# Features split where they are made, and matmul operands at one place modulo 256 bytes

## The chip, the cores and the metric

The kernel runs on one core of a Trainium2 chip, in one launch. The metric is device time in microseconds (us) of one execution. The core has five engines that work side by side, each through its own instructions in order: TensorE (PE) multiplies matrices, with its weight loads shown apart as PEld; VectorE (DVE), ScalarE (ACT) and GpSimd (POOL) work on elements; SyncE (SP) issues most DMA transfers. On-chip memory is a set of 128 partitions, and "place" below means the byte offset of a tile within its partition.

## The reference

Two layers of a decoder trunk act on 1024 prompt tokens and 8 x 8 sample tokens, 1088 rows of width 1024. Layer 0 mixes with an RG-LRU block, layer 1 with an HGRN2 block; each is followed by a feed-forward block with a convolution of width 3 over time (ConvFFN, 2816 features) and each half ends in a layer norm of `ALPHA * x + f(x)`:

```python
def conv_ffn(x, buf, w_in, cw, cb, w_out):
    gate, up = jnp.split(x @ w_in, 2, axis=-1)
    gc, new_buf = causal_dwconv(gate, buf, cw, cb)
    return (jax.nn.gelu(gc) * up) @ w_out, new_buf

def trunk(x, ...):
    for i in range(DEPTH):                       # 2
        mix = rglru_mixer(x, ...) if i % 2 == 0 else hgrn2_mixer(x, ...)
        x = layer_norm(ALPHA * x + mix, ln_g[i, 0], ln_b[i, 0])
        f, fbuf = conv_ffn(x, ffn_conv[i], ffn_w_in[i], ffn_conv_w[i], ffn_conv_b[i], ffn_w_out[i])
        x = layer_norm(ALPHA * x + f, ln_g[i, 1], ln_b[i, 1])
```

All is float32. Besides the rows of both streams, the last states of the mixers and of the convolutions are returned.

## The kernel before, in words

**Split products.** Each operand of a large product is held as two parts in the type fp32r: hi, the value cast, and lo, what the cast left over (value minus hi). A product is three matmuls: hi with hi, hi with lo, lo with hi. A weight tile of 2 x 1024 columns (hi, lo) is made out of a raw tile that a DMA has filled: ACT casts hi, another engine (`run["lo"]`, mostly POOL) subtracts for lo. `convert` does this for a whole tile (lines L220, L221), `convert_part` for half a tile of 512 columns (L189, L190). `pump` asks for the next raw load and makes one such conversion; `fill` and `flush` run small closures that wait in the list `pend`.

**Memory.** `xa` holds the split input of a product as [hi 1088 columns, lo 1088 columns] per block of 128 features. It is one tile under three names: `x` by feature block, `xc[0..3]` as inputs of the up-projection, `yv[0..7]` as eight blocks of features for the down-projection. A tile `x45` holds `xc[4]` and `xc[5]`, later `yv[8..11]`; a tile `x6` holds `xc[6]`. `z` holds the 1088 rows of the residual in float32, nine row tiles of 1024 columns. During the up-projection those rows lie in DRAM (`zsave`), and `z` is cut into eight work slots of 1152 columns (`zslots`). The base weight tiles are `wb0..2` with the raws `raw0, raw1`; each stage adds its own from a pool (`wxf` and `rawf` in the up-projection, `wxb` in the down-projection, `wr` in `mix_out`, which is the output projection of a mixer).

**Order.** The program's order on each engine is written out by hand (`manual_schedule`): a list of steps, each with its weight blocks and a function, run one after another by `run_steps`. An engine takes its instructions in the order in which the functions issue them.

**Up-projection.** The 22 feature blocks are taken in pairs, p = 0 to 10. Each pair has a step `gates` and a step `ups`. Both run `products`: the 2 x 2 blocks of weights and inputs are multiplied in seven products instead of eight, with inputs `xc[0..6]` that are sums of input quarters (`to_sums` writes them), and the seven results are added up in the work slots on evacuation (L1164, L1177 to L1179). Each product comes in two column chunks of 288 and 256 columns (`HCH`; the first holds 32 sample columns), so a step has 7 x 2 x 4 x 3 = 168 matmuls (L1159). The first `gates` step runs `products_first`. Between the products `fills` place other work by (product, chunk): in `ups` the convolution of the gates of the same pair (DVE, then a GELU on ACT); in the next pair's `gates` step `y_mul` of the two blocks, the product of gate and up on DVE, whose result is stored to DRAM (`ysave`, L1230 and L1231) in float32 and whose slots go back. In the last `ups` step there follow `y_load` of blocks 0 to 11 (L1236), `y_part` of the first six, and after the products `y_mul` of the last pair.

**Split on arrival.** `y_part` splits a loaded block in place: two casts on ACT (L1242: 1024 and 64 columns) and two subtractions (L1243), on POOL for odd positions and on DVE for even ones.

**Turn.** A step `turn` between up- and down-projection allocates `wxb`, loads the nine row tiles of `z` back from `zsave` (`load_z`, L653) and puts `y_part` of blocks 6 to 11 into `pend`.

**Down-projection.** The features are taken in four groups (`GROUPS`: blocks 0 to 5, 6 to 11, 12 to 17, 18 to 21). For each group and each half n of the 1024 output columns the nine row tiles m are taken in order; a row tile is 6 x 3 matmuls of 512 columns into one PSUM bank (L1260 to L1262; the sample tile m = 8 takes hi and lo of its 64 rows in one operand and needs 6 x 2, L1265 and L1266), and `resid` adds the bank to `z` on DVE (L463). In the first half of group 0 the first three tiles begin with four blocks each. After a group's second half the group after the next is loaded into the free places, and its `y_part` goes into `pend`. The last group runs within the layer norm.

**What lies where.** The tiles are allocated in order, so that sizes set the places: `xa`, `z`, `gb`, `ident`, `ones`, then 5312 bytes of small tables, then the raws and the base weight tiles. In the up-projection's pool the table `fs` (1584 bytes) stands ahead of `rawf` and `wxf`.

Of the kernel before, what the change touches and what calls it, by code (L numbers as in the profile page):

```python
# [10 lines left out]
F32 = mybir.dt.float32  # L11
FR = mybir.dt.float32r
# [32 lines left out]
HCH = ((0, HD + 256), (HD + 256, 256))  # L45
TW = 1152
# [14 lines left out]
def hawk_hgrn2_convffn_deepnorm_kernel(  # L61
# [27 lines left out]
    ones = cp.tile([P, P], F32, name="ones")  # L89
    ptr = cp.tile([P, KT, 41], F32, name="ptr")  # L90
# [8 lines left out]
    raws = [cp.tile([P, 1024], F32, name=f"raw{i}", tag=f"raw{i}") for i in range(2)]  # L99
    wbase = [cp.tile([P, 2, 1024], FR, name=f"wb{i}", tag=f"wb{i}") for i in range(3)]  # L100
# [266 lines left out]
    def to_sums(mp):  # L367


        if mp < 4:  # L370
            t0, n, ms = HD + mp * P, P, (mp, mp + 4)
# [10 lines left out]
        else:  # L382
            t0, n, ms = 0, HD, (NT - 1,)
# [13 lines left out]
        def put(c, src, eng):  # L397
            hi, lo = (xc[c][:, :, h, t0:t0 + n] for h in range(2))
            act.copy(hi, src)
            eng.tensor_tensor(lo, src, hi, ALU.subtract)  # L400

        def hi_lo(c):
            return (xc[c][:, :, h, t0:t0 + n] for h in range(2))
# [191 lines left out]
    def params_r():  # L595
# [6 lines left out]
        tmp = m1.tile([P, 6, KT], F32, name="ptmp")  # L602
        a, u, q, zz, s, t = (tmp[:, i] for i in range(6))
# [35 lines left out]
    def y_split(m, ks=range(0, KT)):  # L639
        k = slice(ks[0], ks[-1] + 1)  # L640
        if m < NT - 1:
            tk = slice(m * P, (m + 1) * P)
            dst = xm[:, m // 4, k, :, HD + (m % 4) * P:HD + (m % 4 + 1) * P]
            hi, lo = dst[:, :, 0], dst[:, :, 1]
        else:
            tk = slice(SEQ, U)
            hi, lo = ys[:, k, 0], ys[:, k, 1]
# [7 lines left out]
    def mix_out(phase, w, z_src, li, es, early=None):  # L655
# [4 lines left out]
        def prod_part(ps, m, ks, ws, ends=(0, KT - 1)):  # L660
            if m < NT - 1:
                xt = xm[:, m // 4, :, :, HD + (m % 4) * P:HD + (m % 4 + 1) * P]
                for k in ks:
# [3 lines left out]
                    pe.matmul(ps, lhsT=xt[:, k, 0], rhs=wh, start=(k == ends[0]), stop=False)  # L667
                    pe.matmul(ps, lhsT=xt[:, k, 0], rhs=wl, start=False, stop=False)  # L668
                    pe.matmul(ps, lhsT=xt[:, k, 1], rhs=wh, start=False, stop=(k == ends[1]))  # L669
# [108 lines left out]
    def more_weights(es, name, n, kind, side=None):  # L778
        m3 = es.enter_context(tc.tile_pool(name=name, bufs=1, side=side, reuse_waits="tile"))
        wfree[kind].extend(m3.tile([P, 2, 1024], FR, name=f"{name}{i}", tag=f"{name}{i}") for i in range(n))  # L780

# [1149 lines left out]
```

## Time and profile before

| | us |
|---|---|
| three runs | 2563.02, 2563.65, 2564.53 |
| median | 2563.65 |
| the profiled execution, its own time | 2563.38 |
| its span | 2561.6 |
| mixer 0 and what stands ahead of it | 0 to 345 |
| up-projection of layer 0 | 345 to 822 |
| down-projection of layer 0 | 822 to 1060 |
| mixer 1 | 1060 to 1795 |
| up-projection of layer 1 | 1795 to 2272 |
| down-projection of layer 1, with the last layer norm | 2272 to 2561.6 |

The profile comes from one profiled execution. The profile's page gives the busy time of each engine, its share of the span and the number of instructions. Rows of a timeline give the start and length of an instruction, or of a run of equal ones (`x24`), in us from the span's start, its engine, line, operation, `out<-in` by tile names, and shape. Rows of a group give a busy time and the mean length of one instruction in ns. Rows of waits give idle time in us that ended with a release by the named work: the sum, the number of waits, the longest. Rows of a window give its length, the busy time of PE, PEld, DVE, ACT and POOL with instruction counts, the share of full speed that the TensorE clock was granted, the busy share of the DMA engines, and GB/s. Matmuls are pipelined: one of 512 columns is shown with 0.39 us, while the next starts 0.23 us after it; the pace is read from start to start.

### The profile page before, as it was taken

How to read it: one execution, taken by the hardware profiler on the slowest of the kernel's cores; microseconds unless marked ns; L12 is line 12 of the kernel's file. 1: busy time of each engine (PE TensorE's matmuls, PEld its weight loads, DVE VectorE, ACT ScalarE, POOL GpSimd, SP SyncE). 2: the span in 40 equal slices, each digit the busy share in tenths (PEclk: the TensorE clock that was granted, in tenths of full speed). 3: DMA queues.
4: the chain of work that ended last, by engine and by line, in shares of the span. 5: the costliest groups of instructions: out<-in, count | busy, mean ns of one | idle time of the engine just before them, and what ended most of it. 6: DMA issues, size and time to landing. Idle time of an engine off the chain costs nothing. (4 is left out here: it accounts for less than half of the span.)

```text
span 2561.6 us, 39936 instructions
## 1 busy us (share of the span) xinstructions
PE 2496.6 (97%) x16055; PEld 2311.5 (90%) x16055; DVE 1539.0 (60%) x2360; ACT 952.7 (37%) x1659; POOL 1366.3 (53%) x1154
## 2 busy tenths in 40 slices
PE   9999999999999999999999999999999999999997
PEld 8999889999999788799999999878999999988886
DVE  5897476565556322558858485977656565561327
ACT  4776243333334011344444353454423333330113
POOL 2544178888886333025444453623888888862320
PEclk9999999999999999999999999999999999999999
DMA  4114122223224422122111111122222322263112
GB/s 134 42 46 163 42 78 68 85 76 94 85 68 165 144 102 100 41 76 59 51 34 43 51 43 50 44 87 104 75 85 68 102 85 68 85 232 131 59 38 73
DMA packets 205839, 209.79 MB, mean 82 GB/s; under 512 B 13201, under 2 KB 167953, under 8 KB 205614
## 3 DMA queue, kind: packets, MB, share of 16 engines
q1 hardware_dynamic: 205654, 207.25, 25.2%
q8 instruction: 126, 2.06, 0.3%
q14 instruction: 59, 0.48, 0.1%
HBM read 159.61 MB, written 47.61 MB: 81 GB/s over the span
## 5 line engine op out<-in xcount | busy, mean ns | idle before, releaser
L221 POOL TENSOR_TENSOR wb<-raw,wb 128x1024 fp32r<-128x1024 f32 (+1 forms) x75 | 203.2, 2713 | 520.0 <-ACT wb L220 388.9
L1159 PE MATMUL ps_f<-xa,wb 128*128 128x288 f32 x3024 | 390.6, 288 | 1.3 <-ACT z L1179 1.3
L1164 DVE TENSOR_TENSOR z<-z,ps_f 128x256 f32<-128x256 f32 (+2 forms) x520 | 186.2, 380 | 340.7 <-PE ps_f L1159 278.7
L1159 PEld LDWEIGHTS ps_f<-xa,wb 128*128 128x128 f32 x3024 | 384.5, 188 | 1.7 <-ACT z L1179 1.7
L304 PE MATMUL ps_in<-xa,wb 128*128 128x384 f32 (+3 forms) x912 | 306.3, 336 | 10.9 <-ACT y8h L1453 5.9
L305 PE MATMUL ps_in<-xa,wb 128*128 128x384 f32 (+3 forms) x912 | 299.7, 329 | 0.3 <-DVE xa L362 0.3
L306 PE MATMUL ps_in<-xa,wb 128*128 128x384 f32 (+3 forms) x912 | 299.6, 329 | 0.0
L1159 PE MATMUL ps_f<-x,wb 128*128 128x256 f32 (+1 forms) x2304 | 299.1, 289 | 0.0
L1159 PEld LDWEIGHTS ps_f<-x,wb 128*128 128x128 f32 x2304 | 294.1, 189 | 0.2
L463 DVE SCALAR_TENSOR_TENSOR z<-z,ps_fo 128x512 f32<-128x512 f32 x128 | 87.5, 686 | 301.1 <-PE ps_fo L1262 287.3
L190 POOL TENSOR_TENSOR wb<-raw,wb 128x512 fp32r<-128x512 f32 x124 | 177.8, 1443 | 67.9 <-ACT wb L189 66.5
L304 PEld LDWEIGHTS ps_in<-xa,wb 128*128 128x128 f32 x912 | 173.0, 190 | 15.2 <-ACT y8h L1453 7.3
L1210 DVE SCALAR_TENSOR_TENSOR z<-z,ptf 128x1104 f32<-128x1104 f32 x88 | 181.8, 2066 | 1.6
L190 POOL TENSOR_TENSOR wb<-rawf,wb 128x512 fp32r<-128x512 f32 x106 | 148.2, 1403 | 55.2 <-ACT wb L189 49.3
L305 PEld LDWEIGHTS ps_in<-xa,wb 128*128 128x128 f32 x912 | 172.9, 190 | 1.3 <-DVE xa L362 0.7
L306 PEld LDWEIGHTS ps_in<-xa,wb 128*128 128x128 f32 x912 | 172.6, 189 | 0.7
L189 ACT CAST wb<-raw 128x512 fp32r<-128x512 f32 x124 | 75.3, 623 | 201.7 <-POOL raw L185 57.4
L220 ACT CAST wb<-raw 128x1024 fp32r<-128x1024 f32 (+1 forms) x79 | 77.5, 984 | 153.6 <-issue 52.9
L1159 PE MATMUL ps_f<-xa,wxf 128*128 128x288 f32 (+1 forms) x1008 | 133.6, 288 | 0.0
L1260 PE MATMUL ps_fo<-wb,xa 128*128 128x512 f32 x320 | 127.4, 398 | 5.2 <-DVE z L463 5.2
L189 ACT CAST wb<-rawf 128x512 fp32r<-128x512 f32 x106 | 64.7, 623 | 180.3 <-POOL rawf L185 65.9
L1159 PEld LDWEIGHTS ps_f<-xa,wxf 128*128 128x128 f32 x1008 | 129.6, 189 | 0.0
(522 smaller groups left out, 5794.1 us busy)
## 6 DMA issues: line engine op xcount, KB each, us to landing
raw<-in_ffn_w_in_dram SPq DMA_DIRECT2D x48, 512.0 KB
ysave<-z SPq DMA_DIRECT2D x44, 512.0 KB
rawf<-in_ffn_w_in_dram SPq DMA_DIRECT2D x40, 512.0 KB
raw<-in_hg_w_in_dram SPq DMA_DIRECT2D x32, 512.0 KB
xa<-ysave SPq DMA_DIRECT2D x28, 544.0 KB
zsave<-z SPq DMA_DIRECT2D x24, 512.0 KB
rawf<-in_ffn_w_out_dram SPq DMA_DIRECT2D x24, 512.0 KB
z<-zsave SPq DMA_DIRECT2D x24, 512.0 KB
```

The lines of the kernel that those rows point to most:

```text
L189: act.copy(w[:, 0], src)
L190: run["lo"].tensor_tensor(w[:, 1], src, w[:, 0], ALU.subtract)
L220: act.copy(w[:, 0, :n], raw[:, :n])
L221: run["lo"].tensor_tensor(w[:, 1, :n], raw[:, :n], w[:, 0, :n], ALU.subtract)
L304: pe.matmul(ps[:, :n], lhsT=wh, rhs=xh, start=(k == 0), stop=False)
L305: pe.matmul(ps[:, :n], lhsT=wh, rhs=xl, start=False, stop=False)
L306: pe.matmul(ps[:, :n], lhsT=wl, rhs=xh, start=False, stop=(k == KT - 1))
L463: dve.scalar_tensor_tensor(zz, zz, a, ps, ALU.mult, ALU.add, accum_out=stat[:, m, n:n + 1] if acc else None)
L1159: pe.matmul(ps[:, :n], lhsT=l, rhs=r, start=(kk == 0 and i < 4 and l is wh and r is xh), stop=(kk == 3 and l is wl), skip_group_check=(i > ...
L1164: dve.tensor_tensor(d, s, pv(ps), ALU.add)
L1210: dve.scalar_tensor_tensor(c[:, :L], gs[:, i:i + L], w[:, i:i + 1], c[:, :L], ALU.mult, ALU.add)
L1260: pe.matmul(ps, lhsT=yh, rhs=wh, start=a, stop=False)
```

## The change

1. **Where features are split.** `y_part` is gone. `y_hi` (two ACT casts per block) and `y_lo` (two subtractions) stand behind `y_mul` in the next pair's `gates` step, the subtractions on DVE; for the last pair they follow its `y_mul` after the products, the subtractions on POOL. `ysave` has twice the columns and holds prompt hi, sample hi, sample lo and prompt lo; `y_load` loads that. `y_mul` of the second block moves from place (1, 1) to (1, 0).
2. **The turn.** In the last `ups` step only blocks 0 to 5 are loaded, and behind product (5, 1) the row tiles 6, 7 and 8 of `z` (`FREE`); the `turn` step loads the other six row tiles, then blocks 6 to 11. The down-projection takes the row tiles in the order 6, 7, 8, 0 to 5.
3. **Places.** `wb0..2` and the raws are allocated right behind `ones`, ahead of the small tables; `wxf` is the first tile of its pool; four unused tiles fill up (64, 64, 96 and 32 bytes). `xa`, `x45`, the weight tiles and the raws thereby stand at one place modulo 256 bytes.
4. **Columns.** The prompt and sample columns within a hi or lo part of the inputs get another order: `HX` gives the first column of each chunk, apart for hi and lo, and `h_cols` the columns of a row tile. `to_sums`, `y_split` (split for `mix_out`) and `mix_out` use them. An unused helper `put` is taken out.

```diff
+HX = ((256, 0), (0, HD + 256))
+
+def h_cols(q, h):
+    return HX[0][h] if q == 4 else HX[0][h] + HD + q * P if q < 2 else HX[1][h] + (q - 2) * P
...
     ones = cp.tile([P, P], F32, name="ones")
+    wbase = [cp.tile([P, 2, 1024], FR, name=f"wb{i}", tag=f"wb{i}") for i in range(3)]
+    raws = [cp.tile([P, 1024], F32, name=f"raw{i}", tag=f"raw{i}") for i in range(2)]
     ptr = cp.tile([P, KT, 41], F32, name="ptr")
...
+    cp.tile([P, 16], F32, name="pad")
-    ysave = dpool.tile([NF * P, U], F32, name="ysave")
-    raws = ...
-    wbase = ...
+    ysave = dpool.tile([NF * P, 2 * U], F32, name="ysave")
...
         def hi_lo(c):
-            return (xc[c][:, :, h, t0:t0 + n] for h in range(2))
+            return (xc[c][:, :, h, h_cols(mp, h):h_cols(mp, h) + n] for h in range(2))
...
         tmp = m1.tile([P, 6, KT], F32, name="ptmp")
+        m1.tile([P, 16], F32, name="pad1")
...
             if m < NT - 1:
-                xt = xm[:, m // 4, :, :, HD + (m % 4) * P:HD + (m % 4 + 1) * P]
+                xt, xl = (xm[:, m // 4, :, h, h_cols(m % 4, h):h_cols(m % 4, h) + P] for h in range(2))
...
-        more_weights(mo["r"], f"wr{phase}", 2, "r", "right")
+        more_weights(mo["r"], f"wr{phase}", 2, "r", "right", 24)
...
+    FREE = (6, 7, 8)
...
-            fs_["fs"] = fp.tile([P, NF, 18], F32, name=f"fs{li}")
+            wfree["x"].append(fp.tile([P, 2, 1024], FR, name=f"wxf{li}"))
             fs_["raw"] = [fp.tile([P, 1024], F32, name=f"rawf{li}{i}", tag=f"rawf{i}") for i in range(2)]
-            wfree["x"].append(fp.tile([P, 2, 1024], FR, name=f"wxf{li}"))
+            fs_["fs"] = fp.tile([P, NF, 18], F32, name=f"fs{li}")
+            fp.tile([P, 8], F32, name=f"padf{li}")
...
-                    xh, xl = (xc[i][:, kk, h, c0:c0 + n] for h in range(2))
+                    xh, xl = (xc[i][:, kk, h, HX[c][h]:HX[c][h] + n] for h in range(2))
...
-            sp.dma_start(ysave[f * P:(f + 1) * P, NS:], c[:, :SEQ])
-            sp.dma_start(ysave[f * P:(f + 1) * P, :NS], up[:, U:U + NS])
-            T.put(c, up)
+        def y_hi(f):
+            c, up = yst["c", f], yst[f]
+            uf = up.bitcast(FR)
+            act.copy(uf[:, :SEQ], c[:, :SEQ])
+            act.copy(uf[:, SEQ:U], up[:, U:U + NS])
+
+        def y_lo(f, eng):
+            c, up = yst["c", f], yst[f]
+            cf, uf = c.bitcast(FR), up.bitcast(FR)
+            eng.tensor_tensor(cf[:, :SEQ], c[:, :SEQ], uf[:, :SEQ], ALU.subtract)
+            eng.tensor_tensor(uf[:, U:U + NS], up[:, U:U + NS], uf[:, SEQ:U], ALU.subtract)
+            sp.dma_start(ysave[f * P:(f + 1) * P, U + NS:], c[:, :SEQ])
+            sp.dma_start(ysave[f * P:(f + 1) * P, :U + NS], up[:, :U + NS])
+            fs_["T"].put(c, up)

         def y_load(f, i):
-            sp.dma_start(yv[i][:, U:].bitcast(F32), ysave[f * P:(f + 1) * P])
-
-        def y_part(f, i):
-            y = yv[i]
-            for hi, lo in ((y[:, :SEQ], y[:, U + NS:]), (y[:, SEQ:U], y[:, U:U + NS])):
-                act.copy(hi, lo.bitcast(F32))
-                (pool if i % 2 else dve).tensor_tensor(lo, lo.bitcast(F32), hi, ALU.subtract)
+            sp.dma_start(yv[i].bitcast(F32), ysave[f * P:(f + 1) * P])
...
-                    fills = {(0, 1): [lambda: y_mul(f0 - 2)], (1, 1): [lambda: y_mul(f1 - 2)]}
+                    fills = {(0, 1): [lambda: y_mul(f0 - 2)], (1, 0): [lambda: y_mul(f1 - 2)],
+                             (2, 0): [lambda: y_hi(f0 - 2), lambda: y_hi(f1 - 2)],
+                             (3, 0): [lambda: y_lo(f0 - 2, dve)], (3, 1): [lambda: y_lo(f1 - 2, dve)]}
...
-                    for i in range(3, 6):
-                        fills.setdefault((i, 1), []).extend([lambda i=i, j=j: y_load(2 * i + j, 2 * i + j) for j in range(2)])
-                        fills[i, 1].extend([lambda i=i, j=j: y_part(2 * i + j - 6, 2 * i + j - 6) for j in range(2)])
+                    fills.setdefault((5, 1), []).append(lambda: load_z(z_back, FREE))
                 products(b, (u_place(f0), u_place(f1)), fills)
                 if p == NP - 1:
                     y_mul(f0)
                     y_mul(f1)
+                    for f in (f0, f1):
+                        y_hi(f)
+                        y_lo(f, pool)
...
-            load_z(lambda m: zsave[m * P:m * P + rows_of(m)])
+            load_z(z_back, [m for m in range(NT) if m not in FREE])
             load_gb(li, 1)
-            pend.extend([lambda i=i: y_part(i, i) for i in range(6, 12)])
+            for i in range(6, 12):
+                y_load(i, i)
...
-                        for m in range(first):
-                            prod_part(banks[m], m, grp, ws, range(4))
-                        for m in range(NT):
+                        ms = FREE + tuple(m for m in range(NT) if m not in FREE)
+                        for m, ps in zip(ms, banks):
+                            prod_part(ps, m, grp, ws, range(4))
+                        for i, m in enumerate(ms):
...
-                                    pend.append(lambda f=g2 + j, i=j2 + j: y_part(f, i))
```

More of the change, by code (lines that the diff above doesn't have):

```diff
@@ L370, in to_sums @@
         if mp < 4:
-            t0, n, ms = HD + mp * P, P, (mp, mp + 4)
+            n, ms = P, (mp, mp + 4)
             q = []
@@ L642, in y_split @@
             tk = slice(m * P, (m + 1) * P)
-            dst = xm[:, m // 4, k, :, HD + (m % 4) * P:HD + (m % 4 + 1) * P]
-            hi, lo = dst[:, :, 0], dst[:, :, 1]
+            hi, lo = (xm[:, m // 4, k, h, h_cols(m % 4, h):h_cols(m % 4, h) + P] for h in range(2))
         else:
@@ L666, in prod_part @@
                     wl = wt[:, 1, (k % 2) * 512:(k % 2 + 1) * 512]
-                    pe.matmul(ps, lhsT=xt[:, k, 0], rhs=wh, start=(k == ends[0]), stop=False)
-                    pe.matmul(ps, lhsT=xt[:, k, 0], rhs=wl, start=False, stop=False)
-                    pe.matmul(ps, lhsT=xt[:, k, 1], rhs=wh, start=False, stop=(k == ends[1]))
+                    pe.matmul(ps, lhsT=xt[:, k], rhs=wh, start=(k == ends[0]), stop=False)
+                    pe.matmul(ps, lhsT=xt[:, k], rhs=wl, start=False, stop=False)
+                    pe.matmul(ps, lhsT=xl[:, k], rhs=wh, start=False, stop=(k == ends[1]))
             else:
@@ L776, in hawk_hgrn2_convffn_deepnorm_kernel, with more_weights @@
     mo = {}
-    def more_weights(es, name, n, kind, side=None):
+    def more_weights(es, name, n, kind, side=None, pad=0):
         m3 = es.enter_context(tc.tile_pool(name=name, bufs=1, side=side, reuse_waits="tile"))
         wfree[kind].extend(m3.tile([P, 2, 1024], FR, name=f"{name}{i}", tag=f"{name}{i}") for i in range(n))
+        if pad:
+            m3.tile([P, pad], F32, name=f"pad{name}")
     def mix_out_open(phase):
         mo["r"] = ExitStack()
-        more_weights(mo["r"], f"wr{phase}", 2, "r", "right")
+        more_weights(mo["r"], f"wr{phase}", 2, "r", "right", 24)
     def sums_open(es):
@@ L1109, in products_first @@
                             wh, wl = (w[:, a, kk * P:(kk + 1) * P] for a in range(2))
-                            xh, xl = (xc[i][:, kk, a, c0:c0 + n] for a in range(2))
+                            xh, xl = (xc[i][:, kk, a, HX[c][a]:HX[c][a] + n] for a in range(2))
                             for l, r in ((wh, xh), (wh, xl), (wl, xh)):
@@ L1307, in ups, with z_back @@
                     y_mul(f1)
+                    for f in (f0, f1):
+                        y_hi(f)
+                        y_lo(f, pool)
             stepf(phase, [(in_blk(W, f0 * P), in_blk(W, f1 * P))], gates, None if p else "q")
             stepf(phase, [(in_blk(W, DFF + f0 * P), in_blk(W, DFF + f1 * P))], ups)
+        def z_back(m):
+            return zsave[m * P:m * P + rows_of(m)]
         def turn(_):
@@ L1332, in fn @@
                         banks = [sbank("ps_fo") for _ in range(first)]
-                        for m in range(first):
-                            prod_part(banks[m], m, grp, ws, range(4))
-                        for m in range(NT):
-                            if m < first:
-                                prod_part(banks[m], m, grp, ws, range(4, grp[1]))
-                                resid(m, n, banks[m], True)
+                        ms = FREE + tuple(m for m in range(NT) if m not in FREE)
+                        for m, ps in zip(ms, banks):
+                            prod_part(ps, m, grp, ws, range(4))
+                        for i, m in enumerate(ms):
+                            if i < first:
+                                prod_part(banks[i], m, grp, ws, range(4, grp[1]))
+                                resid(m, n, banks[i], True)
                             else:
                                 prod(m, n, grp, ws, gi == 0, False)
-                            if m % 2:
+                            if i % 2:
                                 pump()
```

8 lines of the change are left out of this document (1 added, 7 removed).

## The prediction

> **What bounds the kernel now.** I read the busy table first, then the chain of waits, then the windows by stage.
>
> ```profile
> PE 2496.6 (97%) x16055; PEld 2311.5 (90%) x16055; DVE 1539.0 (60%) x2360; ACT 952.7 (37%) x1659; POOL 1366.3 (53%) x1154
> 1894.30 364.14 PE ps_f L1159 x2892
> 345.00:822.00 477.00, 471.96 (x3728) 470.17 (x3726) 277.30 (x395) 158.77 (x320) 382.45 (x335) 1.00 0.29 90
> ```
>
> PE is busy for 97% of the span. In the up-projection the chain is one unbroken run of 2892 matmuls in 364.14 us, 0.126 us each; the third row (columns: length, then PE, weight load, DVE, ACT, POOL busy, clock, DMA share, GB/s) has POOL at 382 of 477 us there and DVE and ACT with room. So only two things can move the end: moments in which PE stands, and the pace of the matmul stream itself. The change touches both.
>
> The standing is found in the list of waits, the timeline of PE and the clock of short windows around the passage from up- to down-projection ("the turn").
>
> ```profile
> PE ps_fo L1260 <- DVE z L463: 5.2, 2, 3.2
> PE ps_fo L1261 <- POOL wxf L221: 3.9, 2, 2.0
> 820.78 0.39 PE L1260 MATMUL ps_fo<-wb,xa 128*128 128x512 f32 x1
> 866.73 0.39 PE L1260 MATMUL ps_fo<-wb,xa 128*128 128x512 f32 x1
> 2271.76 0.39 PE L1260 MATMUL ps_fo<-wb,xa 128*128 128x512 f32 x1
> 2316.75 0.39 PE L1260 MATMUL ps_fo<-wb,xa 128*128 128x512 f32 x1
> 824.00:828.00 4.00, 3.05 (x7) 1.95 (x8) 4.00 (x5) 3.54 (x7) 4.00 (x3) 0.59 0.42 160
> 844.00:848.00 4.00, 2.21 (x5) 1.82 (x6) 2.95 (x2) 0.00 (x0) 4.00 (x4) 0.65 1.03 418
> ```
>
> Each wait occurs twice, once per layer. The first output half of group 0 is 8 tiles x 18 plus 12 matmuls, 156; at 0.2333 us each (rows further down) that is 36.4 us. It took 866.73 - 820.78 = 45.95 us in layer 0 and 2316.75 - 2271.76 = 44.99 us in layer 1. So the two turns lose 9.55 + 8.6 = **18.1 us**: the waits, and slow matmuls behind each, where the granted clock is 0.59 and 0.65.
>
> **The turn, part by part.** The change removes `y_part` (split on arrival: two ACT casts, two subtractions on DVE or POOL per feature block) and three things that it made late (behind a row in brackets: idle time before it, and what ended it):
>
> ```profile
> 816.21 2.27 ACT L1242 CAST xa<-xa 128x1024 fp32r<-128x1024 f32 x4
> 818.94 1.05 ACT L220 CAST wxf<-rawf 128x1024 fp32r<-128x1024 f32 x1
> 818.41 2.76 POOL L1243 TENSOR_TENSOR xa<-xa 128x1024 fp32r<-128x1024 f32 x2 [4.74 <-ACT xa L1242]
> 821.13 3.34 POOL L221 TENSOR_TENSOR wxf<-rawf,wxf 128x1024 fp32r<-128x1024 f32 x1
> 825.18 2.98 DVE L1243 TENSOR_TENSOR xa<-xa 128x1024 fp32r<-128x1024 f32 x2
> 835.09 2.43 DVE L1229 TENSOR_TENSOR z<-z 128x64 f32<-128x64 f32 x1
> 837.54 0.32 SPq L1231 DMA_DIRECT2D ysave<-z  x1
> 845.05 0.69 DVE L463 SCALAR_TENSOR_TENSOR z<-z,ps_fo 128x512 f32<-128x512 f32 x1 [7.53 <-DMA z<-zsave]
> ```
>
> The second weight block is cast only at 818.94, behind four feature casts, and its low part waits on POOL behind L1243 until 821.13; without these rows both start some 3 us earlier, before PE's first down matmul at 820.78. The splits in the way of the last up-evacuations and `y_mul` on DVE go too: `y_mul` of the last pair, which ended at 835.09 + 2.43 = 837.5, can start about 1 us after the last up matmul.
>
> What is late next is the load of z. The order by hand now begins with tiles 6, 7, 8, whose columns no feature slot of the last pair covers, loaded inside the last ups; they need nothing from the turn. Rows 0 to 5 wait for the last store: from PE's end, 1 us of adds, about 8.9 us for two `y_mul` as slow as the contended ones here, 1.2 us of casts, 2.8 us for the POOL subtraction (the L1243 row), and 7.5 us from the last store to the first add (837.54 to 845.05): 21.4 us. The fifth tile after 6, 7, 8, 0 to 3 needs the bank of tile 0 after 120 matmuls, 27.5 us. So this wait goes with 6 us to spare. If that cover were gone, each us over it costs one us per layer.
>
> The feature loads are twice as long, but six stand ahead of the turn where twelve stood: the same 6.7 MB.
>
> ```profile
> 804.00:808.00 4.00, 4.00 (x35) 4.00 (x34) 0.58 (x2) 1.13 (x1) 0.00 (x0) 1.00 0.99 362
> 816.00:820.00 4.00, 4.00 (x34) 4.00 (x33) 1.36 (x2) 4.00 (x9) 1.59 (x1) 1.00 1.02 406
> ```
>
> At 362 to 406 GB/s a pair of blocks (2.2 MB) takes 5.8 us; the three pairs are released about 18, 15 and 12 us before the turn, so the first four blocks are there 6 us early and the last two at about its start, 7 us before their use. The later loads (6 blocks, 17 us) stand in SP's queue ahead of a weight load, but have a group of 75 us before use. I leave 2 us of the 18.1 for what still comes late: **-16 us**, bounds -8 (only one of the waits goes) and -18.
>
> **The steps added to the up-projection.** Per pair of blocks the gates step gets four casts on ACT (2.3 us by 816.21), and two subtractions with their 64-column parts on DVE, 3.0 us each pair of instructions at worst (825.18). POOL gets them for the last pair alone. Behind `y_hi`, which waits on DVE's `y_mul`, stand the weight casts on ACT; behind `y_lo` DVE's adds.
>
> ```profile
> 709.51 0.62 ACT L189 CAST wxf<-raw 128x512 fp32r<-128x512 f32 x1
> 710.21 1.29 POOL L190 TENSOR_TENSOR wxf<-raw,wxf 128x512 fp32r<-128x512 f32 x1 [1.43 <-ACT wxf L189]
> 727.17 3.17 PE L1159 MATMUL ps_f<-x,wxf 128*128 128x288 f32 x24
> 740.94 0.21 DVE L1229 TENSOR_TENSOR z<-z 128x64 f32<-128x64 f32 x1
> 753.12 0.52 DVE L1164 TENSOR_TENSOR z<-z,ps_f 128x256 f32<-128x256 f32 x2 [4.20 <-PE ps_f L1159]
> ```
>
> A half of a weight tile is complete at 711.5 and used at 727.17: 15.7 us of slack for ACT and POOL. DVE ends `y_mul` at 741.15, early in the step of 21 us, and then has a gap of 4.2 us that takes the subtractions. I cost this at **0**; without that cover it would be up to 5 us in each of 20 gates steps.
>
> **The places.** Sizes in the allocations, taken in order, give the places modulo 256 bytes. Before, xa and z stand at one place, the base weight tiles wb (behind 5312 bytes of small tables) 192 bytes further, wxf and wr elsewhere; the tile x45 that holds features 8 to 11 happens to share wb's place. Afterwards xa, x45 and all weight tiles share one. The down-projection shows shared and unshared places side by side, in one step:
>
> ```profile
> 958.53 0.39 PE L1260 MATMUL ps_fo<-wb,x 128*128 128x512 f32 x1
> 959.88 0.40 PE L1260 MATMUL ps_fo<-wb,xa 128*128 128x512 f32 x1
> 961.28 0.39 PE L1260 MATMUL ps_fo<-wxb,x 128*128 128x512 f32 x1
> 962.67 0.39 PE L1260 MATMUL ps_fo<-wb,x 128*128 128x512 f32 x1
> L1260 PE MATMUL ps_fo<-wb,xa 128*128 128x512 f32 x320 | 127.4, 398 | 5.2 <-DVE z L463 5.2
> L1260 PE MATMUL ps_fo<-wb,x 128*128 128x512 f32 x128 | 49.8, 389 | 0.0
> ```
>
> Six matmuls lie between the first two rows: 1.35 us, 0.2250 each, at one place; the next six, wb against xa, 1.40 us, 0.2333; wxb with x, also at one place, 1.39 us, 0.2317. The group rows agree (398 against 389 ns). So sharing is worth 1.6 to 8.3 ns; I take 5 ns. It comes to wb,xa, wxf,xa, wxb,xa and wxf,x, (320 + 3 x 64) x 3 = 1536 matmuls: **-7.7 us** (-2.5 to -12.8). In mix_out about two thirds of 768 get it, with the new columns: **-2 us** (0 to -6).
>
> In the up-projection the moving operand is the feature, and there nothing shows:
>
> ```profile
> 790.55 9.25 PE L1159 MATMUL ps_f<-x,wb 128*128 128x288 f32 x72
> 799.64 3.18 PE L1159 MATMUL ps_f<-xa,wxf 128*128 128x288 f32 x24
> 802.66 6.20 PE L1159 MATMUL ps_f<-xa,wb 128*128 128x288 f32 x48
> 808.70 3.18 PE L1159 MATMUL ps_f<-xa,wxf 128*128 128x288 f32 x24
> ```
>
> Start to start: 9.09 / 72 = 0.1263 where part of the reads shares a place, 3.02 / 24 and 6.04 / 48 = 0.1258 where none does. Of the new columns, three reads of four share the weights' place and one stands 128 bytes off. I take -0.3 ns x 7056 = **-2 us**; the ends are -32 us (the best of the rows above, in proportion to 272 columns) and +4 us (0.5 ns worse, as in the first row). In the in-projection (2736 matmuls of 384 or 320 columns) no row has the shared place: **-1 us**, ends -23 (8.3 ns each) and +7.
>
> ```profile
> 1278.80 0.28 PE L1760 MATMUL ps_v<-wb,xa 128*128 128x256 f32 x1
> 1279.84 0.28 PE L1760 MATMUL ps_v<-wb,xa 128*128 128x256 f32 x1
> 1294.91 0.28 PE L1765 MATMUL ps_v<-wb,ysh 128*128 128x256 f32 x1
> 1296.11 0.28 PE L1765 MATMUL ps_v<-wb,ysh 128*128 128x256 f32 x1
> ```
>
> The v step speaks against: nine matmuls in 1.04 us (0.1156) at different places, ten in 1.20 us (0.1200) where ysh shares wb's. If that is the place, 768 matmuls lose 4 ns, +3.4 us; I take **+2**, ends -2 and +3.4.
>
> A page speaks against all of this part. The Trainium skill, "SBUF — State Buffer", section Who interferes with whom, says that PE never waits on anyone, and gives places no part in a matmul's pace. By it this part is worth nothing and the sum would be the turn alone. The 1.35 and 1.40 us above do not agree with it.
>
> **The sum.** The profiled execution took 2563.38 us (span 2561.6 and 1.8 around it), 0.3 below the median of 2563.65, so the two can be exchanged. -16 - 7.7 - 2 - 2 - 1 + 2 = -26.7: **2537 us**, own range 2524 to 2549. This measurement can tell about 0.2%, 5 us, from no change.
>
> **The rivals.**
> 1. Places do nothing; the splits of pace above come from which tile it is. Then the turn alone: 2547. For it: the up-projection's 0.126 in every row. Against it: 1.35 and 1.40 us in neighbouring rows of one step. Chance 0.19.
> 2. The turn's stall only moves: rows 0 to 5 of z come late because ACT, DVE and POOL hand the last pair on one after another, and PE stands at tile 4. 10 of the 16 us come back: 2547 as well, with the places in effect. Against it: 6 us to spare. 0.10.
> 3. All shapes gain from the places, the up- and in-projection as much as the best rows: -16 - 12.8 - 6 - 32 - 23 gives 2474 as its end; half of the excess, 2507. 0.09.
> 4. Slower. The shared place is a collision of weight load and moving stream, as the v step reads. At +4.4 ns on 7056 + 2736 + 768 matmuls it costs 46 us and leaves 2563.4 - 16 - 9.7 + 46 = 2584. It decides from 26 / 10560 = 2.5 ns per matmul on; against it, the first of the up rows, partly shared, is only 0.5 ns slower than the others. 0.08.
>
> My forecast has 0.54. The range 2512 to 2556 takes in rivals 1 and 2 and the near part of 3, and leaves out 4 and the far end of 3. Faster by over 0.2%: 0.87 (some of the mild outcomes of 2 and 4 end near no change, 0.05); slower 0.08.
>
> **What would show it.** Right: the waits of L1260 on DVE and L1261 on POOL wxf gone, 36 us between the first matmuls of the two output halves of group 0, clock near 1.00 there; 0.2283 or less per matmul with wb,xa as with wb,x; no L1242 or L1243; up-projection still 0.125 to 0.126. Wrong: PE waits for a weight half (L190) in the gates steps, a wait on z at the turn's fifth or later tile, or 0.130 per up matmul.

## The result and the profile after

| | before | changed | ratio (95% interval) |
|---|---|---|---|
| median, us | 2564.09 (4 runs, 2563.02 to 2566.33) | 2551.36 (4 runs, 2548.38 to 2551.66) | 0.9949 (0.9937 to 0.9961) |
| profiled execution, its own time | 2563.38 | 2551.14 | |
| its span | 2561.6 | 2549.3 | |

The change makes the kernel 12.7 us faster; 26.7 were forecast. The two traces divide cleanly by stage, since PE issues the same 16055 matmuls in both. The table takes the start of PE's first matmul of each stage as its boundary; the last column is the length in the changed kernel less that before.

| stage | before, us | difference, us |
|---|---|---|
| mixer 0 | 339.53 | +4.1 |
| up-projection 0, first step | 35.08 | -1.0 |
| up-projection 0, the 21 steps of `products` | 444.81 | +6.2 |
| down-projection 0, up to mixer 1's first matmul | 284.25 | -15.4 |
| mixer 1 | 688.01 | +2.2 |
| up-projection 1, first step | 33.90 | +0.1 |
| up-projection 1, 21 steps | 444.83 | +6.2 |
| down-projection 1, up to the last matmul | 277.11 | -14.7 |

**What came out as meant.** Windows of the changed kernel (columns as before: length, PE, PEld, DVE, ACT, POOL, clock, DMA share, GB/s), the first around the turn, the second the whole down-projection of layer 0:

```profile
816.00:872.00 56.00, 55.96 (x297) 48.39 (x297) 21.44 (x29) 12.09 (x17) 25.24 (x16) 1.00 0.98 374
822.00:1060.00 238.00, 237.96 (x1086) 197.23 (x1085) 63.04 (x98) 32.70 (x41) 56.19 (x27) 1.00 0.47 174
```

PE does not stand at the turn at all, and its clock stays at 1.00. The groups by shape of the changed kernel say what the places did:

```profile
L1277 PE MATMUL ps_fo<-wb,xa 128*128 128x512 f32 x320 | 124.5, 389 | 0.0
L1277 PE MATMUL ps_fo<-wxf,xa 128*128 128x512 f32 x64 | 24.9, 389 | 0.0
L1169 PE MATMUL ps_f<-xa,wb 128*128 128x256 f32 x1512 | 201.5, 283 | 0.0
```

The matmuls of 512 columns with wb,xa went from 398 to 389 ns, as short as those with wb,x were before. Start to start, that is 0.2330 before and 0.2267 now, and the other pairs of tiles of the down-projection agree with it within about 1 ns. But 256 columns in the up-projection went the other way; the same groups of the kernel before:

```profile
L1159 PE MATMUL ps_f<-xa,wb 128*128 128x256 f32 x1512 | 198.9, 281 | 0.0
```

**What did not.** The list of PE's waits of the changed kernel (in total, times, longest) has a new first line for the steps of `products`; before it stood at 1.3 us in 2 waits:

```profile
PE ps_f L1169 <- ACT z L1189: 4.9, 17, 1.1
```

The timeline of the changed kernel shows one of them, and what led to it:

```profile
2145.74 1.29 POOL L194 TENSOR_TENSOR rawf<-rawf,rawf 128x512 f32<-128x512 f32 x1
2147.06 0.62 ACT L200 CAST wxf<-rawf 128x512 fp32r<-128x512 f32 x1 [2.65 <-POOL rawf L194]
2147.59 1.12 ACT L1224 ACTIVATE z<-z 128x1104 f32<-128x1104 f32 x1
2148.61 0.65 ACT L1189 COPY z<-ps_f 128x288 f32<-128x288 f32 x2
...
2136.60 3.19 PE L1169 MATMUL ps_f<-x,wb 128*128 128x288 f32 x24
...
2145.68 3.19 PE L1169 MATMUL ps_f<-xa,wb 128*128 128x288 f32 x24
2149.04 6.34 PE L1169 MATMUL ps_f<-xa,wb 128*128 128x288 f32 x48 [0.17 <-ACT z L1189]
2167.33 12.27 PE L1169 MATMUL ps_f<-xa,wb 128*128 128x288 f32 x96
2188.52 1.75 PE L1169 MATMUL ps_f<-xa,wxf 128*128 128x288 f32 x12
```

The L1189 copies empty the PSUM bank of product 4 of the `ups` step, whose 24 matmuls (two chunks) start at 2136.60, so that the first chunk is done by 2138.2. ACT gets to them only at 2148.61: in its queue stand ahead of them a GELU and, ahead of that, a weight cast (L200) that waits for a sum on POOL, L194, which POOL began at 2145.74. The bank is needed by product 1 of the next `gates` step, which starts at 2149.04. So this `gates` step, from 2145.68 to 2167.33, takes 21.65 us, and the next `ups` step 21.19. The row shows only 0.17 us idle, because the matmul before it is shown longer than its pace; from start to start that matmul took 0.45 us instead of 0.12, and the one behind it 0.24 instead of 0.13: 0.44 us, nearly the whole difference. Before, the same copies came at 2139.22, some 1.7 us after the first chunk was done:

```profile
2138.19 1.13 ACT L1214 ACTIVATE z<-z 128x1104 f32<-128x1104 f32 x1 [0.55 <-DVE z L1210]
2139.22 0.65 ACT L1179 COPY z<-ps_f 128x288 f32<-128x288 f32 x2
2144.96 9.21 PE L1159 MATMUL ps_f<-xa,wb 128*128 128x288 f32 x72
2166.06 12.25 PE L1159 MATMUL ps_f<-xa,wb 128*128 128x288 f32 x96
2187.21 3.05 PE L1159 MATMUL ps_f<-xa,wxf 128*128 128x288 f32 x23
```

There a `gates` step took 21.10 and an `ups` step 21.15 us. Why POOL is late, the last 400 us of up-projection 1 say, first of the kernel before, then of the changed one:

```profile
1870.00:2270.00 400.00, 399.36 (x3175) 399.15 (x3174) 233.32 (x329) 126.88 (x253) 319.69 (x282) 1.00 0.28 87
```

```profile
1870.00:2270.00 400.00, 397.48 (x3134) 395.66 (x3133) 279.28 (x362) 136.39 (x277) 339.82 (x280) 1.00 0.33 111
```

And of the changed kernel's timeline:

```profile
2135.80 1.29 POOL L201 TENSOR_TENSOR wb<-rawf,wb 128x512 fp32r<-128x512 f32 x1
2139.57 1.59 POOL L201 TENSOR_TENSOR wb<-rawf,wb 128x512 fp32r<-128x512 f32 x1 [0.73 <-ACT wb L200]
2161.66 1.47 DVE L1251 TENSOR_TENSOR z<-z 128x1024 fp32r<-128x1024 f32 x1 [2.84 <-ACT z L1245]
2162.13 2.16 POOL L192 TENSOR_TENSOR raw<-raw 128x512 f32<-128x512 f32 x1
```

POOL issues no more instructions than before, and has 339.82 us of work instead of 319.69: the same kind of sum that takes 1.29 us alone takes 2.16 us beside a subtraction on DVE. The Trainium skill, "SBUF — State Buffer", section SBUF: two separate sides, describes a pair of ports that a DVE instruction with two inputs and a GpSimd instruction hold one at a time, the other waiting; the trace agrees with it in these two lengths. Per pair of steps (2187.21 - 2144.96 = 42.25 us before, 2188.52 - 2145.68 = 42.84 after) POOL is busy for 33.8 us before and 36.4 us after. About 8 times per pair it also waits 0.73 us for ACT's cast of a value that it has just made. 36.4 + 8 x 0.73 = 42.2: POOL has next to nothing left. That this sum is the cause is an argument so far; e4 to e10 test it.

### The profile page after: what moved, and what is told of

Same layout as the page of the kernel before. It is cut to its first block, busy times and chain, and to the rows that moved or that the text cites. A ratio compares the mean times of both kernels' runs of the same rounds, so it can differ in the third digit from the quotient of the medians.

```text
span 2549.3 us, 39949 instructions
## 1 busy us (share of the span) xinstructions
PE 2491.1 (98%) x16055; PEld 2319.3 (91%) x16055; DVE 1583.3 (62%) x2396; ACT 944.4 (37%) x1659; POOL 1348.5 (53%) x1118
## 5 line engine op out<-in xcount | busy, mean ns | idle before, releaser
L1174 DVE TENSOR_TENSOR z<-z,ps_f 128x256 f32<-128x256 f32 (+2 forms) x520 | 175.3, 377 | 140.3 <-PE ps_f L1169 84.9
L201 POOL TENSOR_TENSOR wb<-raw,wb 128x512 fp32r<-128x512 f32 x124 | 200.3, 1626 | 57.9 <-ACT wb L200 57.9
L315 PEld LDWEIGHTS ps_in<-xa,wb 128*128 128x128 f32 x912 | 174.0, 191 | 15.5 <-ACT y8h L1479 7.6
L200 ACT CAST wb<-raw 128x512 fp32r<-128x512 f32 x124 | 75.4, 625 | 218.3 <-POOL raw L196 85.7
L200 ACT CAST wb<-rawf 128x512 fp32r<-128x512 f32 x106 | 64.7, 622 | 212.8 <-POOL rawf L196 78.9
```

The lines of the kernel that those rows point to most:

```text
L200: act.copy(w[:, 0], src)
L201: run["lo"].tensor_tensor(w[:, 1], src, w[:, 0], ALU.subtract)
L315: pe.matmul(ps[:, :n], lhsT=wh, rhs=xh, start=(k == 0), stop=False)
L1174: dve.tensor_tensor(d, s, pv(ps), ALU.add)
```

## The experiments

All times are set against the kernel before on the same chip. Differences are from the profiled executions, against the one of before: "up" is the 42 steps of `products`, "down" both down-projections, "rest" the mixers and the first steps.

| run | median, us | ratio (95% interval) | up | down | rest |
|---|---|---|---|---|---|
| changed kernel | 2551.36 | 0.9949 (0.9937 to 0.9961) | +12.4 | -30.1 | +5.5 |
| e1 split only | 2558.05 | 0.9973 (0.9962 to 0.9983) | +11.3 | -19.0 | +0.1 |
| e2 places only | 2557.65 | 0.9974 (0.9962 to 0.9985) | +2.0 | -11.8 | +3.5 |
| e3 weights 64 bytes off | 2562.19 | 0.9991 (0.9982 to 1.0001) | +11.1 | -21.0 | +9.3 |
| e4 copies on DVE | 2547.30 | 0.9931 (0.9919 to 0.9944) | +6.6 | -29.3 | +8.8 |
| e5 no subtractions | 2539.43 (one run) | | +2.0 | -30.9 | +4.8 |
| e6 no casts | 2545.56 (one run) | | +5.2 | -30.8 | +7.8 |
| e7 one sum on DVE | 2536.25 | 0.9892 (0.9876 to 0.9909) | +0.2 | -30.9 | +3.0 |
| e8 z late | 2566.86 | 1.0014 (1.0004 to 1.0023) | +12.2 | -14.9 | +3.7 |
| e9 before, more on POOL | 2660.31 (one run) | | +86.6 | +5.1 | +5.2 |
| e10 state copies on ACT | 2547.92 | 0.9938 (0.9924 to 0.9952) | +10.2 | -30.2 | +4.5 |
| e11 e7 with inputs moved | 2522.52 | 0.9837 (0.9824 to 0.9850) | -15.5 | -30.9 | +7.0 |
| e12 early rows only | 2557.68 | 0.9978 (0.9968 to 0.9988) | 0.0 | -8.2 | +1.4 |

### e1 and e2: the change in two halves

e1 keeps the split, the turn and the order of row tiles, and takes back places and columns; e2 does the opposite.

```diff
 # e1, against the changed kernel
-HX = ((256, 0), (0, HD + 256))
+HX = ((0, 0), (HD + 256, HD + 256))
-    cp.tile([P, 16], F32, name="pad")
...
```

> Features split where made, turn and order of row tiles as changed; places and columns as before. Theory W (the up-projection is slower because the split work put into the gates steps makes PE wait, and the places are worth their own share elsewhere): each gates step keeps its extra 0.45 to 0.5 us (21.6 us against 21.16), so the two up-projections are 9 to 11 us longer than before; the two down-projections are 18 to 20 us shorter (the turn's stalls alone); 512-column matmuls with wb,xa stay at 0.233; total 2554 to 2557. Rival P (the new places slow the up-projection, and with it the conversions): the gates steps are back at 21.16 us and the total is 2544 to 2546.

> Only the places and the columns of the change; features split on arrival and the turn as before. Theory W: 512-column matmuls at 0.2267 everywhere in the down-projection (11 us less in both, before what the turn's stalls take of it), 256-column matmuls of the up-projection at 0.1197 instead of 0.118 and 288-column ones at 0.1324 instead of 0.133 (together 2.5 to 4 us more), v step 0.120 instead of 0.1168 (2.5 us more), gates and ups steps equal at about 21.19 us; total 2556 to 2559. Rival P: the gates steps show 21.6 us here too, total 2564 to 2567. Rival that the pace goes with the tile and not with its place: 0.233 for wb,xa.

PE's waits of e1, and then of e2:

```profile
PE ps_f L1165 <- ACT z L1185: 6.6, 18, 1.1
```

```profile
PE ps_fo L1267 <- DVE z L467: 6.0, 2, 3.7
...
PE ps_fo L1268 <- POOL wxf L230: 4.0, 2, 2.0
```

e1 has the new waits in the up-projection and none at the turn; e2 has the turn's waits of before and no new ones. Up and down add up: 11.3 + 2.0 against 12.4, 19.0 + 11.8 against 30.1. So theory W holds for where the time went: 11.3 us are lost to the work put into the `gates` steps, whatever the places. The places bring 11.8 us in the down-projections and cost 2.0 in the up-projections. e2's total lies in its range; e1's 2558.05 is 1 us above its own.

### e3: is it the place?

The tile `pad` moves ahead of `wbase`, so that the base weights and raws stand 64 bytes further, and with them the small tables behind them, which are no operands of these matmuls. The inputs, `wxf`, `wxb` and `wr` stay.

```diff
+    cp.tile([P, 16], F32, name="pad")
     wbase = [...]
...
-    cp.tile([P, 16], F32, name="pad")
```

> The changed kernel with the three base weight tiles (and the raws) 64 bytes further; wxf, wxb, wr, xa and x45 stay where they are. If the place modulo 256 bytes sets the pace: wb,xa and wb,x of the down-projection go back from 0.2267 to 0.232 to 0.233 (about 2 x 728 x 6.3 ns = 9 us more), wxf,xa and wxb,xa stay at 0.2267, 256-column matmuls with wb in the up-projection go from 0.1197 to 0.117 to 0.119 (2 to 6 us less) and those with wxf stay at 0.1197; total 2553 to 2559. If it is only the order of the tiles, or their distance from each other, nothing changes: 2551.

Groups of e3 by shape:

```profile
L1277 PE MATMUL ps_fo<-wb,xa 128*128 128x512 f32 x320 | 126.1, 394 | 0.0
L1277 PE MATMUL ps_fo<-wxf,xa 128*128 128x512 f32 x64 | 25.4, 397 | 0.0
L1169 PE MATMUL ps_f<-xa,wb 128*128 128x256 f32 x1512 | 195.6, 279 | 0.0
```

That 64 bytes change the pace in both stages shows that the place counts: wb,xa goes from 389 to 394 ns in the row shown (392 and 390 in the other two of its lines; 0.2267 to 0.2297 from start to start) and from 283 to 279 ns in the up-projection. The rest of the expectation missed: wb,xa did not go back to 0.232, and the total is 2562.19, above the range. wxf,xa stands at the same addresses as in the changed kernel and should have kept its 389 ns; it shows 397 (0.2269 to 0.2315), more than wb,xa, which moved. So the pace is not a property of the one pair of operands. The faster up-projection matmuls brought nothing, since PE then waited longer in the `gates` steps (an `ups` step fell to 20.9 us, a `gates` step rose to 21.9). Together they make 42.8 us, as in e1 and in the changed kernel, though PE's pace is another in each: the length of a pair is not set by the matmuls there.

### e4: the copies out of ACT's queue

```diff
-                        act.copy(d, pv(bk["A"]))
+                        dve.tensor_copy(d, pv(bk["A"])) if up else act.copy(d, pv(bk["A"]))
```

> The changed kernel with the evacuating copies of product 4 of the ups steps on DVE instead of ACT. Theory W1 (PE waits for PSUM banks that these copies release, and the copies stand in ACT's queue behind weight casts that wait for POOL): the waits on the ACT copy go, the gates steps come back from 21.65 to about 21.2 us, 8 to 10 us less in both up-projections, total 2541 to 2544. Rival W2 (POOL's conversions themselves are the bound of the gates steps): PE waits as long, but for the weight halves; 2550 to 2553.

Between the two. The wait on L1189 is gone from the list, but in layer 0 nearly every step stays some 0.1 to 0.2 us too long (21.30 and 21.39 us), now with a bank that DVE's adds (L1174) release late; in layer 1 the steps are so for three pairs and then 21.19 us to the end. So the queue order is how the delay reaches PE. In the later pairs of layer 1 POOL is busy for 36.5 us of 42.37, no less than in the changed kernel, and PE loses nothing. POOL's load alone is thus not what costs time; that its lateness keeps the slow steps of layer 0 alive is argued and not shown.

### e5, e6: which of the added instructions?

```diff
 # e5: y_lo without its two subtractions in the gates steps
-(3, 0): [lambda: y_lo(f0 - 2, dve)], (3, 1): [lambda: y_lo(f1 - 2, dve)]
+(3, 0): [lambda: y_lo(f0 - 2, None)], (3, 1): [lambda: y_lo(f1 - 2, None)]
 # e6: y_hi without its two casts there
+            if f > NF - 3:
                 act.copy(...)
```

> The changed kernel without the subtractions of the features in the gates steps (only the last pair's are left, so that the features' low parts are wrong); casts, stores and order stay. Theory W3 (POOL with its round trips to ACT fills the whole pair of steps: 36.4 us busy and 8 waits of 0.73 us make 42.2 of 42.84 us, because DVE's subtractions stretch POOL's own): POOL falls to about 34.5 us busy per pair, the gates steps to 21.2 us, both up-projections are 4.5 to 5 us shorter than in the changed kernel. Rival W4 (the feature casts on ACT stand ahead of the weight casts and delay those): gates steps stay at 21.6 us.

> The changed kernel without the feature casts on ACT in the gates steps (the last pair's are left, so that the features' high parts are wrong); subtractions, stores and order stay. Theory W3: the gates steps stay at 21.5 to 21.7 us, because POOL is as loaded as before. Rival W4: they fall to about 21.2 us.

The same window as above, of e5 and of e6:

```profile
1870.00:2270.00 400.00, 399.45 (x3143) 397.98 (x3142) 230.95 (x332) 146.72 (x284) 316.54 (x279) 1.00 0.36 122
```

```profile
1870.00:2270.00 400.00, 398.94 (x3160) 398.56 (x3160) 289.60 (x367) 120.60 (x243) 326.74 (x280) 1.00 0.35 117
```

e5 did what W3 expected: 21.19 us for every step but the first few. e6 did what W4 expected: after two slow pairs (22.3 and 22.5 us for the worst steps) it is at 21.19 too. W3's number for e6 was wrong; POOL's work fell there as well, from 339.82 to 326.74, perhaps because DVE's subtractions no longer wait for ACT and meet POOL elsewhere (not shown). Each half of the added work fits alone, and the two together do not. What holds the time is a chain through POOL and ACT with little to spare, and not one of the two instructions.

### e7, e9, e10: POOL relieved, and loaded

```diff
 # e7, in convert_part, product 1
-            pool.tensor_tensor(a21, a11, a21, ALU.subtract)
+            dve.tensor_tensor(a21, a11, a21, ALU.subtract)
 # e9, the kernel before, in convert_part
         run["lo"].tensor_tensor(w[:, 1], src, w[:, 0], ALU.subtract)
+        if b.parts == 7 and i in (0, 4):
+            pool.tensor_tensor(w[:, 1], src, w[:, 0], ALU.subtract)
 # e10, in conv
-                pool.tensor_copy(fs[:, f, 0:2], gs[:, SEQ:SEQ + 2])
+                act.copy(fs[:, f, 0:2], gs[:, SEQ:SEQ + 2])
...
```

> The changed kernel with one of the four raw sums of each step (product 1's, L190) on DVE instead of POOL. Theory W3: POOL loses 2 x 1.3 to 1.8 us per pair, the gates steps come to 21.2 us and both up-projections are 4 to 5 us shorter each, total 2540 to 2544. Rival W2b (ACT's order is the bound whatever POOL does, or DVE becomes late): 21.5 us or more, 2549 to 2553.

> The kernel before with nothing of the change; in each step of the up-projection two of the seven weight subtractions on POOL (products 0 and 4) are issued twice with the same result, 4 x 1.3 us more POOL work per pair. Theory W3 (POOL with its round trips to ACT has only some 2.5 us to spare in a pair of 42.3 us: 33.9 us busy and 8 waits of 0.73 us): each pair becomes 44.5 to 46 us long, each up-projection 22 to 40 us longer, and PE's waits are booked on ACT copies (L1179) or weight halves. Rival (POOL is idle for a fifth of the time and has room): less than 0.5 us per pair, under 5 us per layer.

> The changed kernel with the four small state copies per pair (L1225, L1227) on ACT instead of POOL; DVE's and the features' work stay. Theory W3: POOL is relieved of 2 x (0.73 + 0.19) = 1.8 us per pair, 42.2 falls to 40.4 us, and the gates steps are back at 21.2 us: both up-projections 4 to 5 us shorter each, total 2540 to 2543. Rival (only less work on DVE, or less of what collides with it, helps): gates steps at 21.5 us or more, 2549 to 2552.

The window of e7, then PE's first wait and the window of e9, then the window of e10:

```profile
1870.00:2270.00 400.00, 400.00 (x3136) 398.15 (x3135) 279.11 (x382) 145.85 (x280) 294.68 (x261) 1.00 0.36 123
```

```profile
PE ps_f L1161 <- ACT z L1181: 51.3, 21, 2.8
```

```profile
1870.00:2270.00 400.00, 376.08 (x2892) 372.77 (x2892) 204.12 (x293) 108.22 (x223) 341.56 (x289) 0.97 0.23 68
```

```profile
1870.00:2270.00 400.00, 397.94 (x3139) 396.11 (x3138) 278.68 (x365) 141.99 (x319) 330.87 (x238) 1.00 0.34 114
```

e7: with 294.68 us of POOL work every step of `products` in both layers takes 21.19 us, and PE waits nowhere in them; the total is 4 us below the expected range. DVE issues more instructions than in the changed kernel (382 against 362 in the window), and W2b falls. e9: with none of the change, more work on POOL alone brings the same wait on the same copies (there L1181). A pair became 43.4 / 10.5 = 4.1 us longer, 46.4 us, with 341.56 / 400 x 46.4 = 39.6 us of POOL work, 5.8 more than before. So the kernel before had only some 1.7 us to spare per pair. This is an estimate, and the spare may be larger, since the clock of 0.97 in that window shows that slow matmuls are part of the 4.1 us. The cost was a little above the expected range (43 us per layer against 22 to 40). e10 missed: the `gates` steps came to 21.6 us, not 21.2. POOL's groups show one reason, of the changed kernel and of e10, in the window 450 to 810 us:

```profile
L192 POOL TENSOR_TENSOR rawf<-rawf 128x512 f32<-128x512 f32 x8 | 10.3, 1292 | 0.0
L1225 POOL COPY fs<-z 128x2 f32<-128x2 f32 x16 | 11.6, 725 | 0.0
```

```profile
L192 POOL TENSOR_TENSOR rawf<-rawf 128x512 f32<-128x512 f32 x8 | 18.0, 2245 | 0.6
```

The copy of two columns was booked with 725 ns on average, but took 0.18 us where no DVE instruction with two inputs ran beside it and 1.26 where one did. With the copy gone, the next instruction stands there instead: 2245 ns in place of 1292. So POOL won about 0.9 us per pair and not 1.8. That is not all of it: POOL is busy for some 35.8 us of each later pair in e10 and 35.9 in e6, and e6 has no waits there. In e10 the moved copies stand on ACT itself, right ahead of the copies that PE waits for:

```profile
2144.36 1.12 ACT L1224 ACTIVATE z<-z 128x1104 f32<-128x1104 f32 x1
2145.39 0.17 ACT L1225 COPY fs<-z 128x2 f32<-128x2 f32 x1
2145.47 0.20 ACT L1227 COPY fs<-z 128x16 f32<-128x16 f32 x1
2145.57 0.66 ACT L1189 COPY z<-ps_f 128x288 f32<-128x288 f32 x2
```

L1189 starts 1.21 us after the GELU's start, against 1.02 in the changed kernel (2148.61 - 2147.59). So up to 0.2 of the 0.4 us that a `gates` step still loses may come from the experiment itself, and its miss says little about POOL alone.

### e8, e12: what made the turn short?

```diff
 # e8, against the changed kernel
-                    fills.setdefault((5, 1), []).append(lambda: load_z(z_back, FREE))
-            load_z(z_back, [m for m in range(NT) if m not in FREE])
+            load_z(z_back)
-                        ms = FREE + tuple(m for m in range(NT) if m not in FREE)
+                        ms = tuple(range(NT))
 # e12, the kernel before with the lines that e8 takes out, and nothing else of the change
```

> The changed kernel with all nine row tiles of z loaded at the turn and taken in the order 0 to 8. Theory of the prediction (rows 6, 7, 8 loaded early give the other six the time that they need): four row tiles fill the four PSUM banks after 72 matmuls, 16.3 us, and row 0 comes some 21 us after PE's last up-matmul, so PE stands about 5 us in each turn, and runs some us at a lower clock behind it: each down-projection 4 to 8 us longer than in the changed kernel, total 2559 to 2567. Rival (the split ahead of the turn alone made room): down-projections as in the changed kernel within 1 us.

> The kernel before with the early load of the row tiles 6, 7 and 8 and the order 6, 7, 8, 0 to 5 alone; the split on arrival, the places and the columns stay. e8 showed that without the early rows the split where features are made wins only some 1.5 us per layer at the turn. Theory T1 (two stalls, each with its own cause: z for the fifth row tile, and the split on arrival ahead of the second weight block): PE's waits on DVE z (L463, 5.2 us) go, those on POOL wxf and xa (5.5 us) stay, each down-projection 3.5 to 5 us shorter, total 2554 to 2557. Rival T2 (the two only work together: DVE's subtractions of the split on arrival make the first residual adds late, and z is waited for as before): down-projections within 1.5 us of before, total 2561 to 2565.

PE's longest wait in e8's down-projections, the same in e8's timeline, then the waits of e12:

```profile
PE ps_fo L1277 <- DVE z L469: 10.1, 2, 5.6
```

```profile
850.52 0.79 PE L1277 MATMUL ps_fo<-wb,xa 128*128 128x512 f32 x1 [5.57 <-DVE z L469]
```

```profile
PE ps_fo L1262 <- POOL wxf L221: 3.9, 2, 2.0
PE ps_fo L1262 <- POOL wb L221: 2.5, 2, 1.3
```

Without the early rows PE stands 5.57 us for z, as expected, and the down-projections lose 15.2 of their 30.1 us. With the early rows alone z's wait is gone and those on the conversions stay: -8.2 us, T1's range for the down-projections (the total, 2557.68, is 0.7 above its own). Taken from the places (e8's -14.9 less e2's -11.8) the split alone wins 3.1 us, the early rows alone 8.2, both together 19.0 (e1). The other 7.7 us come only when neither stall is left.

### e11: another place for the inputs of the up-projection

```diff
 # against e7
-    xa = cp.tile([P, KT * 2 * U], FR, name="xa")
+    XS = 48
+    xa0 = cp.tile([P, KT * 2 * U + 64], FR, name="xa")
+    xa = xa0[:, :KT * 2 * U]
-        xc[i] = xa.rearrange(
+        xc[i] = xa0[:, XS:XS + KT * 2 * U].rearrange(
...
```

> As e7 (the changed kernel with product 1's raw sum on DVE), and the seven inputs of the up-projection 192 bytes further within xa, x45 and x6, so that they stand 192 bytes modulo 256 from the weights there, while the features of the down-projection still share the weights' place. If the pace goes with the places and 256 columns like another place than 512 do (0.1157 with weights 64 bytes off in e3): up-projection steps of 20.85 to 21.0 us instead of 21.19, both up-projections together 8 to 14 us shorter than in e7, down-projections as in e7, total 2522 to 2529. If the shared place is best for every matmul: 2536 to 2545.

Groups of e11 by shape, then two rows of its timeline, the starts of two steps:

```profile
L1171 PE MATMUL ps_f<-xa,wb 128*128 128x256 f32 x1512 | 196.0, 279 | 0.0
L1280 PE MATMUL ps_fo<-wb,xa 128*128 128x512 f32 x320 | 124.5, 389 | 0.0
```

```profile
2122.53 9.08 PE L1171 MATMUL ps_f<-xa,wb 128*128 128x288 f32 x72
2143.35 12.06 PE L1171 MATMUL ps_f<-xa,wb 128*128 128x288 f32 x96
```

Every step of `products` takes about 2143.35 - 2122.53 = 20.82 us, a little below the expected range, and the total lies in it. The down-projection keeps its 389 ns, though `xa` is 256 bytes longer here and the base weights stand that much further from its features. This version beats both kernels: 2522.52 us, 41 less than before.

## Why the prediction was wrong

**The step that failed** is "The steps added to the up-projection", costed at 0. Measured: +11.3 us (e1), in nearly every one of the 20 `gates` steps some 0.5 us and in the first of each layer about 1. Two readings in it were wrong. The slack of 15.7 us was read from one half of a weight tile, its end against its use; but PE never waited for weights. It waited for a PSUM bank, through copies that stand on ACT behind casts that depend on POOL. And POOL, at 382 of 477 us, was given no part in the cost; the prediction counts its subtractions of the last pair alone. Its round trips to ACT belong to its load, and with them it had little left per pair (some 1.7 us by e9's estimate). The gap of 4.2 us on DVE did take the subtractions, but they stretched POOL's own. Taking away DVE's subtractions (e5), ACT's casts (e6) or one sum of POOL (e7) each brought the steps back, and with the copies off ACT POOL's full load fitted (e4, layer 1). So the loss comes along the chain from POOL over ACT's queue to the bank; how much of its lateness belongs to POOL and how much to ACT stays open. The prediction named a sign of being wrong in these steps (a wait for a weight half, L190), and the sign that came was another one.

**The turn, -16.** Right in mechanism, and 1 us beyond the end of -18: -19.0 (e1), of which 17.6 are in the two first output halves and the rest was not traced. In the changed kernel the two output halves of group 0 begin 35.76 us apart in both layers, where 36 were named as the sign. The 6 us to spare for rows 0 to 5 held, since nothing waits for z. Rival 2 (the stall only moves) is what e8 shows without the early rows.

**Places in the down-projection, -7.7.** Right in mechanism, too small: 6.3 ns instead of 5 on most of the 1536 matmuls, some 10 us. e2's -11.8 is 2 us more, which was not traced. Rival 1 (places do nothing) falls with e3: the first matmul of each three with wb,xa took 398, 389 and 394 ns at three places of wb. The Trainium skill, "SBUF — State Buffer", section Who interferes with whom, says that PE never waits on anyone. Whether PE ever waits for another engine's access was not tested here; that places are worth nothing, as the prediction read it, does not agree with these rows.

**The other places.** In the up-projection the forecast was -2, and it came to +2.0 (e2), inside the ends given: 256 columns lost 1.5 ns and 288 won 0.9 (0.1182 to 0.1197, 0.1334 to 0.1325, from start to start), which makes 2.1 us over 3528 of each. The v step, also 256 columns, lost 2.4 us (+2 forecast). `mix_out` won about 1.7 (-2). The in-projection's pace stayed as it was (-1). Rival 4 (the shared place a collision for all) was right for 256 columns only, and at 1.5 ns below its point of 2.5. Rival 3 (all shapes gain) falls with it; half of its excess, by its own terms, would have been about 2505 and not 2507.

**What was in no sum.** Some 2.7 of mixer 0's +4.1 us are the clock. Both kernels wait 2.8 us there for the same ACT instruction. Windows behind it, of the changed kernel, then of the one before:

```profile
197.50:202.80 5.30, 5.30 (x19) 5.30 (x18) 5.30 (x4) 5.27 (x8) 5.30 (x2) 0.50 0.09 24
```

```profile
195.50:200.80 5.30, 5.30 (x34) 5.30 (x33) 5.30 (x4) 5.27 (x8) 5.30 (x2) 1.00 0.07 15
```

After the same pause one execution ran at half clock for 5.3 us and the other at full clock. The Trainium skill, "TensorE: Matmul & The Clock Gate", section Part 1: The HAM clock gate, says that the windows which decide this run freely and do not start with the kernel; these two windows agree. "Rest" in the table lies between +3.0 and +8.8 in the runs with the changed kernel's places (e2, e4 to e8, e10 among them) and between 0 and +5.2 in those with the places of before (e1, e9, e12), though the mixers are the same within each kind; part of that may be such luck, and the v step's 2.4 us are in it. What else is in it was not tried.

In short: gains of 30 us where 24 were forecast at turn and places together, and 11 us given back in the steps that the split was moved to, which stood at 0 in the sum.

## What to carry to other kernels

Count an engine's load in a repeated step with its round trips to other engines, and look for what stands behind its results in another engine's queue: an engine at 80% can have little to spare. Where two engines slow each other down, work moved to the idle one is paid by the busy one, and an instruction's booked time can be the wait of whichever comes next. Place the operands of each stage for themselves: what is best for 512 columns is not best for 256.

## What the runs showed of the hardware that was not expected

With the operands at one place modulo 256 bytes (but for the low part of the 288-column inputs, 128 bytes off) the pace of the up- and down-projection is uniform: 0.2267 us for 512 columns, 0.1325 for 288, 0.1197 for 256. With other places 512 columns are slower (0.230 to 0.233) and 256 are mostly faster (down to 0.116 in e3 and e11). It does not go with the pair of operands alone: wxf,xa at the same two addresses took 389 ns in the changed kernel and 397 in e3, where its neighbours in the stream stand elsewhere. What the rule behind this is stays open, and so does the period: a shift of 256 bytes changed nothing in e11's down-projection, 64 did in e3, and 128 was not tried by itself.

The up-projection has two states that keep themselves. In e4 one layer stayed at 21.30 and 21.39 us per step and the other, with the same instructions, got back to 21.19 after three pairs and remained there; in e6 both did. In both layers of e4 the first `gates` step took 22.51 us, so what decides between the two states was not found; in e4 it is worth 2.2 us of a layer's up-projection.
